# Input projections of a hybrid attention/state-space layer: loads on SyncE's queue, stores on ScalarE's, a third sum tile, and v's second columns after two products

## The chip, the cores and the metric

The kernel runs on one core of one Trainium2 chip. The metric is the time on the device in microseconds (us); a time is the median of several runs. Five engines work side by side, each through its own instructions in order: TensorE (PE, matrix products, with a weight load ahead of each), VectorE (DVE), ScalarE (ACT), GpSimd (POOL) and SyncE (SP), which here only starts transfers (DMAs). ScalarE can start transfers too; such a start stands in its queue among its other instructions, and waits there for what it needs, as they do.

## The reference

One layer on 2048 tokens of 1024 features, all in float32:

```python
h = rms_norm(x, norm_gain)
z = h @ w_in                       # 1024 x 5120
q, k, v, gate_a, u_s, gate_s, merge_logits = split(z)
q, k = rms_norm(q per sub-head), rms_norm(k per sub-head)
o_a = diff_attention(q, k, v, ...) * silu(gate_a)
o_s = s5_branch(u_s, ...) * silu(gate_s)
g_a, g_s = split(sigmoid(merge_logits + merge_gate_b))
x + (g_a * (o_a @ proj_attn) + g_s * (o_s @ proj_ssm)) @ w_out
```

q, k, v, gate_a, u_s and gate_s have 512 columns each, the merge logits 2048. The attention has four heads with two sub-heads of 64 features.

## The kernel before

Each product is made of three, as both factors are split into a coarse part in a short float format (`hh`, `w[0]`) and the rest (`hl`, `w[1]`): high by high, high by low, low by high (`split3`, L38 to L42). A product here is 128 columns of `w_in` by a block of 512 tokens, over 8 slices of the 1024 features: 24 matmuls of 128x512 into one PSUM bank (`proj1`, L206). v is made the other way round, 128 tokens by 256 columns, 24 matmuls of 128x256 (`value`, L250).

The first phase, `phase1`, makes z in this order:

- The input of block t, `load_x` (L167): eight tiles `xs` (tag "x", four buffers) are loaded; ScalarE makes `hh`, VectorE `hl`, ScalarE squares (tag "q", two buffers), GpSimd adds the squares up in `acc` (tag "t", two buffers, L175 and L177). `acc` is split (`sh`, `sl`, tag "s"), summed over the partitions by two matmuls with a matrix of ones (`msx`, L194 and L195), and gives `E` and, for each token, the factor `rc` (L201) that v's evacuation needs (L260).
- Two groups g of q and v columns, four blocks of tokens t in each. In a block, `qk` makes two q products with v's products between them: `n` (L288) says how many of the block's four v's come after the first and after the second. In group 0 the next block's input is made between these products. After the first product the norm of the block before is done (`later`, L229): `ms` (L235, L236), `tt` (tag "t", L238), logarithm and exponential on ScalarE and three operations on VectorE (`newton`, L91), then the two halves of q (L244): the first into a further tile of tag "t", the second into `tt` itself. Each half is split (`hilo`, a cast on ScalarE, a subtraction on VectorE, L864 and L866), and both parts are stored (L247, L248).
- Weights come through raw tiles (`wraw`, three buffers, 256 KB a load): for v by `load_w` (L126; load L135, cast L139, rest L140), for all other columns by `steps_w1` (L150; load L156, cast L160, rest L161). v's weights fill all four buffers of their tag, so the second group's overwrite the first's.
- Two groups of k with the state-space input u (`state`, L303; store L310) in the place of v.
- After `mid()`, which makes the state-space branch, 24 columns of gates (`gate`, L335): product, a factor, Silu or Tanh, store (L352).

All PSUM tiles of these products share six banks (L111); `msx` and `ms` have two of their own. Weight loads, and input loads from block 1 on, are started by ScalarE; all stores, and the input loads of block 0, by SyncE. The order of the instructions on each engine isn't the order of the text: a list scheduler with a model of the times works it out when the program is built, and so mixes v's products into q's, or the state-space branch into the gates. Buffers of a tag are handed out in the order of the text.

Of the kernel before, what the change touches and what calls it, by code (L numbers as in the profile page):

```python
# [17 lines left out]
NTB = 4  # L18
# [26 lines left out]
def block_ones(nc, k, c, bo):  # L45
    nc.gpsimd.memset(bo, 0.0)
    for i in range(0, 128, 32):
        nc.gpsimd.memset(bo[i:i + 32, i:i + 32], 1.0 / 64)
    k.bones = c.tile([128, 128], F32R, name="bones")
    nc.vector.tensor_copy(k.bones, bo)  # L50
    nc.gpsimd.memset(bo, 1.0)
    nc.vector.tensor_copy(k.ones, bo)


def consts(tc, k, I):
    nc = tc.nc
    nc.scalar.preload_act_table_set("natural_log_exp_and_others")
    c = k.cp
    k.ident = c.tile([128, 128], F32, name="ident")
    k.ones = c.tile([128, 128], F32R, name="ones")  # L60
    with tc.tile_pool(name="c0", bufs=1, side="right", reuse_waits="tile") as c0:
        block_ones(nc, k, c, c0.tile([128, 128], F32, name="bo"))
    small = c.tile([128, 8 + 2 + 2 + 16 + 1 + 4], F32, name="small")
    nc.sync.dma_start(small, I["small"])
    k.gain = small[:, 0:8]
    k.qg = c.tile([128, 2], F32, name="qg")
    nc.vector.tensor_scalar(out=k.qg, in0=small[:, 8:10], scalar1=-0.125, scalar2=None, op0=ALU.mult)
    k.kg = small[:, 10:12]
    k.hmb = c.tile([128, 16], F32, name="hmb")
    nc.vector.tensor_scalar(out=k.hmb, in0=small[:, 12:28], scalar1=0.5, scalar2=None, op0=ALU.mult)  # L70
    k.sgain = c.tile([128, 1], F32, name="sgain")
    nc.vector.tensor_scalar(out=k.sgain, in0=small[:, 28:29], scalar1=0.8 * 128 ** 0.5, scalar2=None, op0=ALU.mult)
    k.mhalf = c.tile([128, 2], F32, name="mhalf")
    nc.gpsimd.memset(k.mhalf, -0.5)
    k.hglub = c.tile([128, 4], F32, name="hglub")
    nc.vector.tensor_scalar(out=k.hglub, in0=small[:, 29:33], scalar1=0.5, scalar2=None, op0=ALU.mult)
# [25 lines left out]
def phase1(tc, k, I, mid):  # L102

    nc = tc.nc
    with ExitStack() as es:
# [13 lines left out]

        BUFS = {"x": 4, "s": 2, "q": 2, "t": 2, "n": 2, "o": 2, "v": 2}  # L120
        W = {}
# [4 lines left out]
        def load_w(g, eng=None):  # L126

            W[g] = []
            for i in range(4):
# [4 lines left out]
                o = slice(2 * (i % 2), 2 * (i % 2) + 2)  # L134
                nc.scalar.dma_start(raw, I["win"][g][:, 2 * i:2 * i + 2])  # L135
                if eng:
# [13 lines left out]
        def steps_w1(c, tag, eng=None):  # L150
            w = wh, wl = [k.wp.tile([128, 8, 128], F32R, tag=tag, bufs=4, name="w1") for _ in range(2)]
            yield w
            for i in range(2):
                raw = k.wp.tile([128, 4, 128], F32, tag="wraw", bufs=3, name="wraw")
                o = slice(4 * i, 4 * i + 4)
                nc.scalar.dma_start(raw, I["win"][c // 2][:, o, 128 * (c % 2):128 * (c % 2) + 128])  # L156
                if eng:
# [9 lines left out]
        def load_x(t):  # L167
# [11 lines left out]
            for kk in range(8):  # L179
                xs[kk] = et("x", "xs")  # L180
                (nc.scalar if t else nc.sync).dma_start(xs[kk], I["xT"][kk * 128:(kk + 1) * 128, t * TB:(t + 1) * TB])
                gc = k.gain[:, kk:kk + 1]
# [10 lines left out]
            hilo(nc, sh, acc, sl)  # L193
            nc.tensor.matmul(ms, k.ones, sh, start=True, stop=False)  # L194
            nc.tensor.matmul(ms, k.ones, sl, start=False, stop=True)  # L195
            e, r = E[:, t * TB:(t + 1) * TB], rc[:, 4 * t:4 * t + 4]
# [12 lines left out]

        def qk(w, t, gcol, dst, between):  # L210


            ps, sq = [], []
            for i in range(2):
                ps.append(pm.tile([128, TB], F32, tag="pm", name="ps_qk"))
                proj1(w[i], t, ps[i])
                sq.append(et("q", "sq"))
                nc.scalar.activation(out=sq[i], in_=ps[i], func=AF.Square)
                between(i)
                if i == 0:  # L220
                    later()
            nc.vector.tensor_tensor(out=sq[0], in0=sq[0], in1=sq[1], op=ALU.add)
            sh, sl = et("s", "sh", F32R), et("s", "sl", F32R)
# [5 lines left out]
        def later():  # L229
            if pending:  # L230
                pending.pop()()

        def qk_norm(t, gcol, dst, ps, sh, sl):
# [8 lines left out]
            for i in range(2):  # L242
# [3 lines left out]
                hilo(nc, qh, q, eng=nc.vector)  # L246
                nc.sync.dma_start(f(dst[i, 0, :, :, ts]), f(qh))  # L247
                nc.sync.dma_start(f(dst[i, 1, :, :, ts]), q)  # L248

        def value(g, b):  # L250
# [9 lines left out]
            nc.scalar.activation(out=v, in_=ps.rearrange("p (h d) -> p h d", h=2), func=AF.Copy, scale=rc[:, b:b + 1])  # L260
            nc.sync.dma_start(k.VT[g - 4][:, :, b].rearrange("h p d -> p h d"), v)

# [5 lines left out]
        with ExitStack() as e1:  # L268
# [13 lines left out]
            for g in range(2):  # L282
# [3 lines left out]
                for t in range(NTB):  # L286
                    x = load_x(t + 1) if g == 0 and t + 1 < NTB else iter(())
                    n = (4, 0) if t == NTB - 1 else (2, 2)  # L288
                    b = iter(range(4 * t, 4 * t + 4))
# [6 lines left out]

                    qk(w, t, k.qg, k.QT[g], between)

            for g in range(2, 4):
# [3 lines left out]
                def state(i, t):  # L303
# [5 lines left out]
                    nc.vector.tensor_tensor(out=u[:, ::-1].rearrange("p a c -> p c a"), in0=v(ps), in1=v(R), op=ALU.mult)  # L309
                    nc.sync.dma_start(k.US[2 * (g - 2) + i][:, :, 64 * t:64 * t + 64], u)  # L310

# [23 lines left out]
        def gate(c, ts, w=None, ps=pst):  # L335

            w = w or load_w1(c, "wh" if c == cols[0] else "wl")
            for t in ts:
# [12 lines left out]
                if t == ts[-1] or t % 2:  # L351
                    nc.sync.dma_start(dst[:, t0 * TB:(t + 1) * TB], z[:, 0:t + 1 - t0])  # L352
            return w
# [880 lines left out]
```

## Time and profile before

| | |
|---|---|
| median of 3 runs | 1773.14 us (1772.15 to 1774.92) |
| profiled execution | 1772.99 us, its span 1771.2 us |
| TensorE busy | 1691.9 us, 96% of the span |
| VectorE, ScalarE, GpSimd busy | 1032.2, 699.7, 285.8 us |
| mean granted TensorE clock | 0.986 of full speed |
| moved by DMA | 239.05 MB, 135 GB/s |

The profile is one execution. Stages by what TensorE does: q and v to about 246 us, k and u to about 419 us, the gates to about 990 us (with the state-space branch between them), then the attention and the projections of the result. A wait row reads: the engine and line that waited, the engine and line that ended the wait, total us, number of waits, the longest. A timeline row reads: start and duration in us, engine, line, operation, result and operands; a bracket at its end is idle time of that engine just before.

### The profile page before, as it was taken

To read this page: it belongs to the slowest core of one execution; us is meant where nothing else is said; L and a number is where in the kernel's file an instruction comes from. 1 tells how busy PE (TensorE), PEld (TensorE's weight loads), DVE (VectorE), ACT (ScalarE), POOL (GpSimd) and SP (SyncE) were. 2 spreads that over 40 slices of the span, in tenths; PEclk is the share of its full clock that TensorE was granted. 3 is DMA by queue.
4 is the path that set the end of the run, shared out by engine and by line. 5 is a ranking of instruction groups with operands and counts; after the bars stand their busy time and mean duration, and the time that the engine had idled before them with its cause. 6 is when DMAs were issued, how large, how long until landed. Compare 5 with 4: busy or idle time off the path is not lost.

```text
span 1771.2 us, 24819 instructions
## 1 busy us (share of the span) xinstructions
PE 1691.9 (96%) x8720; PEld 1426.8 (81%) x8720; DVE 1032.2 (58%) x2564; ACT 699.7 (40%) x1426; POOL 285.8 (16%) x428
## 2 busy tenths in 40 slices
PE   7877999999999999999999789999999989999999
PEld 6776988888878788888888668878888879888887
DVE  7533345545734359999644587687677668643331
ACT  4533232324312243331144577675555466511100
POOL 3421000000260000000023335552111032100000
PEclk9888999999999999999999899999999999999999
DMA  5333233424343433323465764753754534654532
GB/s 166 94 92 97 67 107 78 114 76 117 103 127 121 130 119 115 110 95 100 131 203 190 237 202 144 230 169 110 221 173 127 160 103 131 196 162 148 149 101 83
DMA packets 225405, 239.05 MB, mean 135 GB/s; under 512 B 56032, under 2 KB 166016, under 8 KB 224256
## 3 DMA queue, kind: packets, MB, share of 16 engines
q1 hardware_dynamic: 182656, 210.19, 39.1%
q10 hardware_dynamic: 42624, 27.27, 5.4%
q8 instruction: 69, 1.13, 0.3%
q14 instruction: 56, 0.46, 0.1%
HBM read 146.44 MB, written 90.96 MB: 134 GB/s over the span
## 4 chain that ended last, share of the span: by engine, by line
PE 70%; DMA 13%; DVE 7%; ACT 3%; POOL 3%; issue 3%; SPq 1%; ACTq 0%; POOLq 0%; DVEq 0%
PE ps_p L40 9%; PE ps_p L41 9%; PE ps_p L42 9%; PE ps_o L575 5%; PE ps_o L40 3%; PE ps_o L42 3%; PE ps_o L41 3%; PE ps_s L536 2%; PE ps_s L535 2%; PE ps_qk L40 2%; PE ps_qk L41 2%; PE ps_qk L42 2%; PE ps_t L567 2%; DMA xs<-xT 2%; PE ps_u L42 1%
## 5 line engine op out<-in xcount | busy, mean ns | idle before, releaser
L42 PE MATMUL ps_p<-hh,w 128*128 128x512 f32 x768 | 300.3, 391 | 0.0
L40 PE MATMUL ps_p<-hh,w 128*128 128x512 f32 x768 | 300.2, 391 | 0.0
L41 PE MATMUL ps_p<-hl,w 128*128 128x512 f32 x768 | 300.1, 391 | 0.0
L41 PEld LDWEIGHTS ps_p<-hl,w 128*128 128x128 f32 x768 | 144.2, 188 | 30.1 <-issue 0.7
L42 PEld LDWEIGHTS ps_p<-hh,w 128*128 128x128 f32 x768 | 144.3, 188 | 29.5 <-issue 0.4
L40 PEld LDWEIGHTS ps_p<-hh,w 128*128 128x128 f32 x768 | 144.3, 188 | 29.0 <-issue 0.5
L548 ACT ACTIVATE e<-e,mm 128x640 f32<-128x640 f32 (+11 forms) x96 | 136.2, 1419 | 60.5 <-DVE mm L546 59.6
L575 PE MATMUL ps_o<-V,at 128*128 128x128 f32 x1088 | 149.9, 278 | 2.9 <-ACT sq L581 2.2
L575 PEld LDWEIGHTS ps_o<-V,at 128*128 128x128 f32 x1088 | 143.0, 194 | 9.7 <-ACT sq L581 2.8
L535 PE MATMUL ps_s<-K,Q 128*128 128x512 f32 (+3 forms) x320 | 129.5, 408 | 10.4 <-DMA Q<-Q 5.9
L538 DVE TENSOR_SCALAR_CACHE_REDUCE e<-ps_s 128x512 f32<-128x512 f32 (+1 forms) x192 | 120.4, 641 | 27.6 <-PE ps_s L536 26.5
L40 PE MATMUL ps_qk<-hh,w 128*128 128x512 f32 x256 | 102.5, 400 | 15.6 <-ACT hh L183 8.4
L536 PE MATMUL ps_s<-K,Q 128*128 128x512 f32 (+3 forms) x320 | 115.7, 365 | 1.2 <-DMA Q<-Q 1.1
L344 DVE TENSOR_TENSOR z<-ps_p,E 128x512 f32<-128x512 f32 x96 | 66.1, 688 | 75.2 <-PE ps_p L42 74.3
L41 PE MATMUL ps_qk<-hl,w 128*128 128x512 f32 x256 | 102.3, 400 | 4.2 <-DVE hl L184 4.2
L42 PE MATMUL ps_qk<-hh,w 128*128 128x512 f32 x256 | 101.4, 396 | 0.0
L350 ACT ACTIVATE z<-z,hmb 128x512 f32<-128x512 f32 x64 | 46.2, 723 | 124.3 <-DVE z L344 111.8
L567 PE MATMUL ps_t<-ident,e 128*128 128x128 f32 x544 | 84.7, 273 | 9.1 <-DVE e L558 3.8
L558 DVE SCALAR_TENSOR_TENSOR e<-e,cf 128x128 f32<-128x128 f32 (+7 forms) x64 | 90.1, 1407 | 1.2
L256 PE MATMUL ps_v<-w,hh 128*128 128x256 f32 x256 | 75.7, 298 | 10.2 <-ACT w L139 6.8
L569 ACT COPY at<-ps_t 128x512 f32<-128x512 f32 (+3 forms) x160 | 78.8, 520 | 16.7 <-PE ps_t L567 16.5
L567 PEld LDWEIGHTS ps_t<-ident,e 128*128 128x128 f32 x544 | 65.7, 141 | 22.0 <-ACT at L569 6.0
(346 smaller groups left out, 3691.8 us busy)
## 6 DMA issues: line engine op xcount, KB each, us to landing
wraw<-win ACTq DMA_DIRECT2D x80, 256.0 KB
TM<-z SPq DMA_DIRECT2D x32, 512.0 KB
u<-US SPq DMA_DIRECT2D x64, 128.0 KB
K<-K SPq DMA_DIRECT2D x8, 1024.0 KB
Q<-Q SPq DMA_DIRECT2D x32, 256.0 KB
Q<-Q SPq DMA_DIRECT2D x64, 128.0 KB
t<-TM SPq DMA_DIRECT2D x32, 256.0 KB
MS<-t SPq DMA_DIRECT2D x32, 256.0 KB
```

What stands on the lines that cost most here:

```text
L40: nc.tensor.matmul(out, wh, xh, start=start, stop=False)
L41: nc.tensor.matmul(out, wh, xl, start=False, stop=False)
L42: nc.tensor.matmul(out, wl, xh, start=False, stop=stop)
L256: nc.tensor.matmul(ps, xh, wh, start=kk == 0, stop=False)
L535: nc.tensor.matmul(ps, Q[:, 0, s, 128 * b:128 * b + 128], Kt[s][:, ks], start=True, stop=False)
L536: nc.tensor.matmul(ps, Q[:, 1, s, 128 * b:128 * b + 128], Kt[s][:, ks], start=False, stop=True)
L538: nc.vector.tensor_scalar(out=et[:, ks], in0=ps, scalar1=0.0, scalar2=3e38, op0=ALU.add, op1=ALU.min, accum_out=mc[:, i:i + 1])
L548: nc.scalar.activation(out=et, in_=et, func=AF.Exp, bias=mm, scale=-1.0, accum_out=su)
L558: nc.vector.scalar_tensor_tensor(out=e[0], in0=e[1], scalar=cf, in1=e[0], op0=ALU.mult, op1=ALU.add)
L567: nc.tensor.transpose(pt[:, x], e[:, o:o + 128], k.ident)
L569: nc.scalar.copy(AT[g][:, :w], pt[:, :w])
L575: nc.tensor.matmul(po, AT[x // 4][:, x % 4], Vt[x // 8][:, x % 8], start=x == 0, stop=x == n - 1)
```

## The change

- Input and weight loads (L135, L156, L181) are all started by SyncE; the stores of q and k (L247, L248), v (L261), u (L310) and gates (L352) by ScalarE.
- Tag "t" gets a third buffer. The matrix of ones keeps 32 of its 128 columns, and `msx` reads its first column 128 times over.
- In block 0 of the second group, both q products come before all four v's (`n` is (0, 4), not (2, 2)), and the norm of the block before is done after the second product, ahead of the v's.

```diff
--- before.py
+++ after.py
@@ -49,7 +49,7 @@
     k.bones = c.tile([128, 128], F32R, name="bones")
     nc.vector.tensor_copy(k.bones, bo)
     nc.gpsimd.memset(bo, 1.0)
-    nc.vector.tensor_copy(k.ones, bo)
+    nc.vector.tensor_copy(k.ones, bo[:, 0:32])
 
 
 def consts(tc, k, I):
@@ -57,7 +57,7 @@
     nc.scalar.preload_act_table_set("natural_log_exp_and_others")
     c = k.cp
     k.ident = c.tile([128, 128], F32, name="ident")
-    k.ones = c.tile([128, 128], F32R, name="ones")
+    k.ones = c.tile([128, 32], F32R, name="ones")
     with tc.tile_pool(name="c0", bufs=1, side="right", reuse_waits="tile") as c0:
         block_ones(nc, k, c, c0.tile([128, 128], F32, name="bo"))
     small = c.tile([128, 8 + 2 + 2 + 16 + 1 + 4], F32, name="small")
@@ -117,7 +117,7 @@
         E = rp.tile([128, T], F32, name="E")
         rc = k.cp.tile([128, 16], F32, name="rc")
 
-        BUFS = {"x": 4, "s": 2, "q": 2, "t": 2, "n": 2, "o": 2, "v": 2}
+        BUFS = {"x": 4, "s": 2, "q": 2, "t": 3, "n": 2, "o": 2, "v": 2}
         W = {}
 
         def et(tag, name, dtype=F32):
@@ -132,7 +132,7 @@
                     W[g].append((wh, wl))
                 raw = k.wp.tile([128, 2, 256], F32, tag="wraw", bufs=3, name="wraw")
                 o = slice(2 * (i % 2), 2 * (i % 2) + 2)
-                nc.scalar.dma_start(raw, I["win"][g][:, 2 * i:2 * i + 2])
+                nc.sync.dma_start(raw, I["win"][g][:, 2 * i:2 * i + 2])
                 if eng:
                     eng.tensor_copy(wh[:, o], raw)
                 else:
@@ -153,7 +153,7 @@
             for i in range(2):
                 raw = k.wp.tile([128, 4, 128], F32, tag="wraw", bufs=3, name="wraw")
                 o = slice(4 * i, 4 * i + 4)
-                nc.scalar.dma_start(raw, I["win"][c // 2][:, o, 128 * (c % 2):128 * (c % 2) + 128])
+                nc.sync.dma_start(raw, I["win"][c // 2][:, o, 128 * (c % 2):128 * (c % 2) + 128])
                 if eng:
                     eng.tensor_copy(wh[:, o], raw)
                 else:
@@ -178,7 +178,7 @@
 
             for kk in range(8):
                 xs[kk] = et("x", "xs")
-                (nc.scalar if t else nc.sync).dma_start(xs[kk], I["xT"][kk * 128:(kk + 1) * 128, t * TB:(t + 1) * TB])
+                nc.sync.dma_start(xs[kk], I["xT"][kk * 128:(kk + 1) * 128, t * TB:(t + 1) * TB])
                 gc = k.gain[:, kk:kk + 1]
                 nc.scalar.activation(out=hh[t][:, kk], in_=xs[kk], func=AF.Copy, scale=gc)
                 nc.vector.scalar_tensor_tensor(out=hl[t][:, kk], in0=xs[kk], scalar=gc, in1=f(hh[t][:, kk]),
@@ -191,8 +191,8 @@
             ms = k.pF.tile([128, TB], F32, tag="F", bufs=k.NF, name="msx")
             sh, sl = et("s", "sh", F32R), et("s", "sl", F32R)
             hilo(nc, sh, acc, sl)
-            nc.tensor.matmul(ms, k.ones, sh, start=True, stop=False)
-            nc.tensor.matmul(ms, k.ones, sl, start=False, stop=True)
+            nc.tensor.matmul(ms, k.ones[:, 0:1].to_broadcast([128, 128]), sh, start=True, stop=False)
+            nc.tensor.matmul(ms, k.ones[:, 0:1].to_broadcast([128, 128]), sl, start=False, stop=True)
             e, r = E[:, t * TB:(t + 1) * TB], rc[:, 4 * t:4 * t + 4]
             nc.vector.tensor_scalar(out=e, in0=ms, scalar1=EPS / 1024, scalar2=EPS * EPS, op0=ALU.mult, op1=ALU.add)
             sq = et("q", "sq")
@@ -207,7 +207,7 @@
             for kk in range(8):
                 split3(nc, ps, w[0][:, kk], w[1][:, kk], hh[t][:, kk], hl[t][:, kk], kk == 0, kk == 7)
 
-        def qk(w, t, gcol, dst, between):
+        def qk(w, t, gcol, dst, between, last=0):
 
 
             ps, sq = [], []
@@ -216,9 +216,12 @@
                 proj1(w[i], t, ps[i])
                 sq.append(et("q", "sq"))
                 nc.scalar.activation(out=sq[i], in_=ps[i], func=AF.Square)
-                between(i)
                 if i == 0:
+                    between(i)
+                if i == last:
                     later()
+                if i:
+                    between(i)
             nc.vector.tensor_tensor(out=sq[0], in0=sq[0], in1=sq[1], op=ALU.add)
             sh, sl = et("s", "sh", F32R), et("s", "sl", F32R)
             hilo(nc, sh, sq[0], sl, nc.vector)
@@ -244,8 +247,8 @@
                 nc.vector.scalar_tensor_tensor(out=q, in0=ps[i], scalar=gcol[:, i:i + 1], in1=tt, op0=ALU.mult, op1=ALU.mult)
                 qh = et("o", "qh", F32R)
                 hilo(nc, qh, q, eng=nc.vector)
-                nc.sync.dma_start(f(dst[i, 0, :, :, ts]), f(qh))
-                nc.sync.dma_start(f(dst[i, 1, :, :, ts]), q)
+                nc.scalar.dma_start(f(dst[i, 0, :, :, ts]), f(qh))
+                nc.scalar.dma_start(f(dst[i, 1, :, :, ts]), q)
 
         def value(g, b):
             t, o = b // 4, (b % 4) * 128
@@ -258,7 +261,7 @@
                 nc.tensor.matmul(ps, xl, wh, start=False, stop=kk == 7)
             v = k.ep.tile([128, 2, 128], F32, tag="v", bufs=BUFS["v"], name="v")
             nc.scalar.activation(out=v, in_=ps.rearrange("p (h d) -> p h d", h=2), func=AF.Copy, scale=rc[:, b:b + 1])
-            nc.sync.dma_start(k.VT[g - 4][:, :, b].rearrange("h p d -> p h d"), v)
+            nc.scalar.dma_start(k.VT[g - 4][:, :, b].rearrange("h p d -> p h d"), v)
 
         def steps(it, n=1):
             for _ in range(n):
@@ -285,7 +288,7 @@
                     steps(load_w(5), 4)
                 for t in range(NTB):
                     x = load_x(t + 1) if g == 0 and t + 1 < NTB else iter(())
-                    n = (4, 0) if t == NTB - 1 else (2, 2)
+                    n = (4, 0) if t == NTB - 1 else (0, 4) if g and not t else (2, 2)
                     b = iter(range(4 * t, 4 * t + 4))
 
                     def between(i):
@@ -294,7 +297,7 @@
                             value(4 + g, next(b))
                         steps(x, 1 + 8 * i)
 
-                    qk(w, t, k.qg, k.QT[g], between)
+                    qk(w, t, k.qg, k.QT[g], between, int(n[0] == 0))
 
             for g in range(2, 4):
                 w = [load_w1(2 * g + i, "wh") for i in range(2)]
@@ -307,7 +310,7 @@
                     proj1(wu[i], t, ps)
                     v = lambda x: x.rearrange("p (c a) -> p c a", a=8)
                     nc.vector.tensor_tensor(out=u[:, ::-1].rearrange("p a c -> p c a"), in0=v(ps), in1=v(R), op=ALU.mult)
-                    nc.sync.dma_start(k.US[2 * (g - 2) + i][:, :, 64 * t:64 * t + 64], u)
+                    nc.scalar.dma_start(k.US[2 * (g - 2) + i][:, :, 64 * t:64 * t + 64], u)
 
                 for t in range(NTB):
                     R = et("x", "R")
@@ -349,7 +352,7 @@
                     dst = k.TM[c - 24]
                     nc.scalar.activation(out=zi, in_=zi, func=AF.Tanh, scale=0.5, bias=k.hmb[:, c - 24:c - 23])
                 if t == ts[-1] or t % 2:
-                    nc.sync.dma_start(dst[:, t0 * TB:(t + 1) * TB], z[:, 0:t + 1 - t0])
+                    nc.scalar.dma_start(dst[:, t0 * TB:(t + 1) * TB], z[:, 0:t + 1 - t0])
             return w
 
         cols = (12, 13, 14, 15, 20, 21, 22, 23, *range(24, 40))
```

## The prediction

> **What bounds the kernel now.** I read the page first: TensorE (PE) and its granted clock in tenths, each digit a fortieth of the span, some 44 us.
>
> ```profile
> span 1771.2 us, 24819 instructions
> ...
> PE   7877999999999999999999789999999989999999
> ...
> PEclk9888999999999999999999899999999999999999
> ```
>
> PE is at 9 nearly everywhere; the weak places are the first four digits and the two at about 1000 us. The same in numbers, from the busy times by stretches (columns: stretch, its length, then busy us and instruction count of PE, weight loads, VectorE, ScalarE, GpSimd, then clock, DMA share, GB/s), first by stage, then for the weak part of the first:
>
> ```profile
> core 0: us, PE busy (x) PEld busy (x) DVE busy (x) ACT busy (x) POOL busy (x), PEclk, DMA share, GB/s
> 0.00:246.00 246.00, 208.70 (x1196) 182.95 (x1197) 107.82 (x184) 98.70 (x178) 49.93 (x47) 0.94 0.37 104
> 246.00:419.00 173.00, 173.00 (x763) 143.00 (x762) 91.22 (x134) 47.14 (x83) 0.00 (x0) 1.00 0.36 95
> 419.00:990.00 571.00, 568.69 (x2649) 470.28 (x2649) 353.37 (x1021) 187.60 (x350) 73.10 (x100) 1.00 0.43 132
> ```
>
> ```profile
> 20.00:160.00 140.00, 113.77 (x637) 99.37 (x637) 63.03 (x116) 62.06 (x114) 42.16 (x32) 0.89 0.37 107
> ```
>
> All that the diff touches lies in the projections and gates, up to 990 us. From 246 us PE is busy 741.7 of 744 us there: nothing to win, only to lose. The stretch that can give time is 20 to 160 us, the normalised input, q's first columns and v. There PE stands 140 - 113.8 = 26.2 us, and its clock is 0.89, so 0.11 x 113.8 = 12.5 us more go in slow matmuls: 38.7 us in all. The first 20 us I leave out. Who made PE stand (columns: engine and line that waited, releaser, total us, times, longest):
>
> ```profile
> PE ps_qk L40 <- ACT v L260: 7.3, 2, 6.4
> PE ps_v L256 <- ACT w L139: 6.8, 2, 4.9
> PE ps_v L256 <- ACT v L260: 3.4, 1, 3.4
> PE msx L194 <- ACT sh L864: 2.9, 2, 1.8
> PE msx L195 <- POOL sl L866: 1.9, 3, 0.9
> PE ps_qk L40 <- ACT hh L183: 1.5, 1, 1.5
> PE ps_v L257 <- POOL w L140: 1.3, 2, 1.0
> PE ms L236 <- DVE sl L866: 1.0, 1, 1.0
> ```
>
> The rows add up to 26.1, the whole of it. I put them in three causes. **Ring**: the first row, 7.3 us. **Weights of v's second columns**: L139 and L140, 8.1 us. **Input sums**: the other five, 10.7 us. The clock loss follows the gaps: after each, the clock falls for some us.
>
> ```profile
> 64.00:68.00 4.00, 4.00 (x19) 4.00 (x20) 3.76 (x4) 1.97 (x4) 1.72 (x1) 0.50 0.66 133
> 84.00:88.00 4.00, 4.00 (x22) 3.72 (x22) 4.00 (x14) 1.98 (x5) 0.00 (x0) 0.64 0.10 9
> ```
>
> So I charge each us of gap 12.5 / 26.1 = 0.48 us of clock: a factor of 1.48. Ring 10.8, weights 12.0, sums 15.8.
>
> On this clock the Trainium skill speaks ("TensorE: Matmul & The Clock Gate", section "What's actually happening"): the gate closes only after an idle window of about 3.4 us, and stays closed about as long. By that rule only the three longest gaps would pay a half-speed window of about 1.7 us each, 5 us in all, and the two that the forecast below removes would pay 3.4 us, not 7.4, so that it would be 4 us smaller. The row at 84 us, 0.64 after two gaps that were each under 2 us, speaks against so clean a line.
>
> **Third tile for sums and values.** The tag "t" holds the input's sum (acc), the norm's value (tt) and the first half of q. With two tiles they wait for each other and for the stores out of them. VectorE's timeline:
>
> ```profile
> 64.74 0.69 DVE L99 SCALAR_TENSOR_TENSOR tt<-nw_a,nw_y 128x512 f32<-128x512 f32 x1
> ...
> 83.77 0.74 DVE L244 SCALAR_TENSOR_TENSOR q<-ps_qk,qg,tt 128x512 f32<-128x512 f32 x1
> ...
> 86.71 0.68 DVE L866 TENSOR_TENSOR q<-q,qh 128x512 f32<-128x512 f32 x1
> ...
> 87.74 0.68 DVE L866 TENSOR_TENSOR tt<-tt,qh 128x512 f32<-128x512 f32 x1
> ```
>
> The waits of VectorE (20 to 165 us) and of ScalarE (0 to 165 us):
>
> ```profile
> DVE tt L238 <- DMA Q<-tt: 11.3, 1, 11.3
> DVE w L161 <- ACT w L160: 9.1, 2, 5.3
> DVE tt L238 <- DMA Q<-q: 8.6, 1, 8.6
> ```
>
> ```profile
> ACT hh L183 <- DMA xs<-xT: 20.9, 17, 4.1
> ACT nw_y L95 <- DVE tt L238: 10.7, 3, 8.4
> ACT w L139 <- DMA wraw<-win: 9.3, 3, 4.8
> ACT acc L175 <- DMA Q<-q: 7.8, 1, 7.8
> ACT hh L183 <- DVE w L137: 4.9, 3, 3.0
> ```
>
> tt is ready at 65.4, but q is made at 83.8, because its tile is still the next block's sum. Then the stores of both must land before acc (7.8) and tt (11.3) of later blocks can start; ScalarE takes its queue in order, so v's evacuation (L260) comes late and PE, out of PSUM banks, waits. That is the 6.4 us, and the same a block later, tt waiting 8.6 and ScalarE's nw_y behind it 8.4, makes the 0.9 left of the row. With three tiles the order acc, acc, acc, tt, q gives q a tile that the first block's sum left long ago, and the stores have a whole block, over 20 us, to land. I take all of the ring away: -10.8. Bounds: 0 if some other wait stands right behind it, and -10.8 less 2.7 x 1.48 = 4.0 more if the two msx gaps of the last block (1.8 and 0.9 are the longest of their rows) go with it, as that block's sum began 7.8 us late. What is late next: the input's sums, which are costed below.
>
> **v's second columns half a product later.** In the first block of the second group both q products now come before the four v's. The weights of v's second columns reuse the tiles of the first, so their casts can't start before the last v of the first group; the row of L139 shows that ScalarE stood 9.3 us for their loads as well, 4.8 at a time: three raw tiles, two of them held by the q columns' weights. The edit puts one product more in front. A product is 24 matmuls; in the second stretch above, where PE never stands, 763 instructions took 173.0 us, 0.227 each, so 24 x 0.227 = 5.4 us of cover against 8.1 us of waits. The other 2.7 us: these casts stand on ScalarE behind the nw_y that the ring held for 8.4 us, so the ring's end gives back more than that. I take the weights' whole 12.0 away; bounds -8.0 (5.4 x 1.48) and -12.0. The previous block's norm is put off with it (later() after the second product): two PSUM banks stay taken 5.4 us longer, of six, and the four v's that would need them come after it. Nothing.
>
> **Loads to SyncE.** 24 input loads and 80 weight loads leave ScalarE's queue. ScalarE no longer stands where such a load waits for its buffer; it stands where the data is late. In the rows of L183 the 4.9 us, where the load in front waited for VectorE, go. The 20.9 us mostly stay: the input has four tiles before and after, and a load can only start when a square has freed one, on whichever queue it stands. What the gaps of the sums (15.8) lose is therefore between 0 and all; I take -2, the nearest row being the 4.9, of which the part before 20 us gives nothing here. On SyncE the loads now queue behind each other alone: input tile 4 of the first block waits for VectorE, with weight loads behind it; before, the weights were on the other queue. I take 0, bounds -1 and +2. The rule against this edit is in the Trainium skill ("DMA: Bandwidth & Descriptors", section "Issuing engines are not separate DMA queues"): transfers interleave on the same 16 DMA engines whatever queue starts them, and only issue time is saved. By it the -2 would be 0 and the sum 2 us higher. No run shown so far can separate the two.
>
> **Stores to ScalarE.** Per norm four stores, per v, u and gate one. A store of ScalarE's own result waits for its end only. But the second and fourth wait for VectorE's subtraction. ScalarE's casts ahead of them:
>
> ```profile
> 84.55 0.62 ACT L864 CAST qh<-q 128x512 fp32r<-128x512 f32 x1 [0.59 <-DVE q L244]
> ...
> 86.41 0.62 ACT L864 CAST qh<-tt 128x512 fp32r<-128x512 f32 x1
> ```
>
> By these and VectorE's two subtractions above, qh ends at 85.17, the subtraction at 87.39, 2.2 us; then 87.03 to 88.42, 1.4 us. Behind them on ScalarE stand the next casts, input tiles, squares and v. That is 3.6 us a norm, where ScalarE is the link that the sums run through: four norms in the first group, 14.4 us. Most of it falls where ScalarE is idle (62.1 busy of 140): I take +4, bounds 0 and 14.4 x 1.48 = 21.3. From 246 us ScalarE is busy 47.1 of 173 and then 187.6 of 571, PE has six banks of cover: 0. SyncE in turn no longer stands before the state-space loads; PE is full there: 0.
>
> **Shorter ones.** The sums of the input use the shorter tile of ones:
>
> ```profile
> L194 PEld LDWEIGHTS msx<-sh,ones x4: 186/186/188, 27.8 to 118.9; 128*128 128x128 f32 x4
> ```
>
> Four times two such weight loads now read one column broadcast; even at twice the price 8 x 0.19 = 1.5 us, in the gaps. I take 0.
>
> **Sum.** -10.8 - 12.0 - 2 + 4 = -20.8 on the profiled execution's own 1772.99 us (its span 1771.2 and 1.8 around it; the runs' median is 1773.14, the same within 0.2): 1752.2, say **1752 us**. After 160 us everything hangs on PE's order, so it all moves forward together: the state-space work starts when this stage gives its tiles back, and the weak stretch at 1000 us comes as much earlier.
>
> **Rivals.** About 0.2%, 3.5 us, is what a measurement here can tell from no change.
>
> *A, the forecast*: ring and weights go, sums stay. Its own range 1744 to 1761. Chance 0.52.
>
> *B, the sums go too*: q made 18 us earlier frees PSUM, ScalarE freed of loads makes the input tiles in time, and all 38.7 us go but the stores' 4: 1738. For it: 20.9 us of ScalarE waiting for input. Against: the four input tiles and the square's two tiles are as before, and the x sum is emitted in the same place of PE's order. Chance 0.14.
>
> *C, half is given back*: only one of the two is gained, as the other's stall is taken over by the sums (the next block's sum is no earlier than before), or the stores cost half their bound: -20.8 + 10 gives 1762. Chance 0.14.
>
> *D, nothing*: the stores' upper 21.3 eats the 22.8: 1771. This is also the case that the change doesn't do what it says, for instance because the order of each engine's instructions, worked out anew for the changed queues, puts the input loads behind weight loads that wait for a tile. Chance 0.08.
>
> *E, slower*: ScalarE stands before VectorE's subtractions in the second group as well. Of the 16 norms of q and k, each exposed one costs 3.6 x 1.48 = 5.3; the gain of 24.8 without the stores' term is used up from the fifth exposed one on. With eight exposed, 42.6: 1773.0 - 24.8 + 42.6 = 1791. For it: one in-order queue now holds casts, logarithms and waiting stores. Against: PE full for 741.7 of 744 us with ScalarE a third busy. Chance 0.12.
>
> **How the numbers follow.** Faster by over 0.2%: A, B and C, 0.80. Same: D, 0.08. Slower: E, 0.12. The range takes in A, B and C: from B's 1738 to 1768, C with the rest of the stores' bound.
>
> **What would show it.** Right: no wait of tt or acc for a store of q; q within 2 us of tt in the first block; PE's waits for L139 and L140 under 1 us; PE idle in 20 to 140 us down from 26 to about 11 us, at msx, ms and v after an input sum; the first state product at about 225 instead of 246 us; PE full from there to about 970. Wrong: waits of ScalarE, or of the store queue, for the subtraction (L866) over 10 us in the first 140 us with hh or v behind them; PE gaps between 246 and 990 us; or a hand-over at 1000 us with more than the idle time it has now.

## The result and the profile after

The change is faster, by less than forecast: 1760.38 us as the median of 4 runs (1755.97 to 1762.6), beside 1772.89 us for the kernel before on the same chip. The ratio is 0.9925, 95% interval 0.9903 to 0.9946, that is 13.3 us of 1773 (9.6 to 17.2). The profiled execution took 1762.6 us, its span 1760.7. Line numbers from L210 on are 1 to 3 higher than before: `later` calls L238 and L239, q is made at L247, v evacuated at L263, the split stands at L867 and L869.

In the page's rows of TensorE and of its clock, the fourth digit of the first row rose from 7 to 9, the second and fourth of the clock by one each, and the weak place at about 1000 us stayed:

```profile
span 1760.7 us, 24771 instructions
...
PE   7879999999999999999999799999999999999998
...
PEclk9989999999999999999999899999999999999999
```

The stretches of the first stage, with the columns of the prediction:

```profile
0.00:246.00 246.00, 217.04 (x1240) 191.09 (x1241) 116.30 (x193) 100.65 (x182) 50.77 (x47) 0.94 0.38 110
20.00:160.00 140.00, 122.83 (x700) 109.08 (x700) 71.86 (x128) 63.86 (x118) 40.96 (x30) 0.90 0.39 110
```

Between 20 and 160 us PE stands 140 - 122.8 = 17.2 us where it stood 26.2. But the clock is 0.90, where it was 0.89: by the prediction's reckoning 0.10 x 122.8 = 12.3 us go in slow matmuls, about as many as before (12.5). Who makes PE stand there:

```profile
PE ps_v L259 <- ACT v L263: 7.6, 3, 3.4
PE msx L194 <- ACT sh L867: 7.6, 2, 7.4
PE ms L239 <- DVE sl L869: 1.2, 2, 0.7
PE msx L195 <- POOL sl L869: 0.6, 1, 0.6
PE ms L238 <- ACT sh L867: 0.2, 1, 0.2
```

The row of the ring (ps_qk, 7.3) and those of v's weights (L139 and L140, 8.1) are gone; what is left, 17.2 us, are the sums and the v behind them, 10.7 before. VectorE's timeline shows the ring open: tt is ready at 65.5, and q follows at 67.1, not 18 us later.

```profile
64.77 0.69 DVE L99 SCALAR_TENSOR_TENSOR tt<-nw_a,nw_y 128x512 f32<-128x512 f32 x1
...
67.07 0.74 DVE L247 SCALAR_TENSOR_TENSOR q<-ps_qk,qg,tt 128x512 f32<-128x512 f32 x1
```

ScalarE's waits up to 165 us have a new kind, "issue": time in which it waits for nothing that the profile shows, here right behind stores in its own queue.

```profile
ACT hh L183 <- issue: 4.2, 1, 4.2
ACT acc L175 <- DMA Q<-q: 3.4, 1, 3.4
...
ACT v L263 <- issue: 3.1, 1, 3.1
...
ACT sq L175 <- issue: 2.5, 2, 2.1
```

Those are 9.8 us of standing that did not exist before (its waits there had no row of "issue"), on the engine that the sums run through. The obvious reading is that the stores on ScalarE ate the missing 8 us. It was my first theory, and it fell.

### The profile page after: what moved, and what is told of

Read it like the earlier page. It is cut to its first block, busy times and chain, and to the rows that moved or that the text cites. A ratio compares the mean times of both kernels' runs of the same rounds, so it can differ in the third digit from the quotient of the medians.

```text
span 1760.7 us, 24771 instructions
## 1 busy us (share of the span) xinstructions
PE 1693.2 (96%) x8720; PEld 1433.1 (81%) x8720; DVE 1027.7 (58%) x2564; ACT 702.6 (40%) x1426; POOL 284.0 (16%) x428
## 4 chain that ended last, share of the span: by engine, by line
PE 68%; DMA 13%; DVE 6%; ACT 4%; POOL 4%; issue 3%; SPq 1%; ACTq 0%; POOLq 0%; DVEq 0%
PE ps_p L40 9%; PE ps_p L42 9%; PE ps_p L41 9%; PE ps_o L578 3%; PE ps_o L42 3%; PE ps_o L40 3%; PE ps_o L41 3%; PE ps_qk L41 3%; PE ps_qk L42 3%; PE ps_qk L40 3%; PE ps_a L40 2%; PE ps_a L41 2%; PE ps_a L42 2%; PE ps_u L40 2%; PE ps_u L41 2%
## 5 line engine op out<-in xcount | busy, mean ns | idle before, releaser
L544 DVE CUSTOM_DVE_ANT_0 e<-ps_s,nb 128x384 f32<-128x384 f32 (+3 forms) x128 | 70.0, 553 | 19.5 <-PE ps_s L539 15.7
```

## The experiments

All ratios are to runs of the kernel before on the same chip. The groups ran on different chips, so ratios are to be compared across them, not medians. "us" is (ratio - 1) x 1773; "u" is the start of the first state product in the profiled execution.

| kernel | ring | v's columns | loads | stores | median us | ratio, 95% interval | us | u |
|---|---|---|---|---|---|---|---|---|
| the change | new | new | SP | ACT | 1760.38 | 0.9925 (0.9903 to 0.9946) | -13.3 | 236.5 |
| e1 | new | | ACT | SP | 1752.02 | 0.9877 (0.9857 to 0.9896) | -21.8 | 233.7 |
| e2 | | new | ACT | SP | 1767.30 | 0.9970 (0.9956 to 0.9983) | -5.3 | 244.3 |
| e3 | new | new | ACT | SP | 1752.13 | 0.9879 (0.9862 to 0.9896) | -21.5 | 232.2 |
| e4 | | | SP | ACT | 1771.02 | 0.9987 (0.9973 to 1.0001) | -2.3 | 242.7 |
| e5 | new | new | SP | SP | 1757.35 | 0.9906 (0.9889 to 0.9924) | -16.7 | 238.7 |
| e6 | new | new | ACT | ACT | 1769.81 | 0.9978 (0.9963 to 0.9992) | -3.9 | 241.1 |
| e8 | new | new | SP | q, k: SP; rest ACT | 1765.51 | 0.9953 (0.9938 to 0.9969) | -8.3 | 238.1 |
| e9 | own sum tile | | ACT | SP | 1766.64 | 0.9963 (0.9949 to 0.9976) | -6.6 | 240.3 |
| e10 | new | new | ACT | q, k, v: ACT; rest SP | 1770.49 | 0.9976 (0.9963 to 0.9988) | -4.3 | 243.4 |
| e11 | new | new | ACT | u, gates: ACT; rest SP | 1766.53 | 0.9953 (0.9935 to 0.9970) | -8.3 | 230.6 |
| e12 | new | new | SP | ACT, order of e3 | 1754.94 | 0.9885 (0.9864 to 0.9906) | -20.4 | 233.1 |
| e13 | new | new | ACT | SP, order of the change | 1759.29 | 0.9913 (0.9897 to 0.9929) | -15.4 | 237.7 |

### The parts one by one (e1 to e4)

e1 is the kernel before with the third tile (and the short tile of ones that makes room for it); e2 only has v's columns half a product later; e3 has both, on the old queues; e4 has only the loads and stores moved.

```diff
-        BUFS = {"x": 4, "s": 2, "q": 2, "t": 2, "n": 2, "o": 2, "v": 2}
+        BUFS = {"x": 4, "s": 2, "q": 2, "t": 3, "n": 2, "o": 2, "v": 2}
```

> The third tile of tag t alone (with the shorter tile of ones that goes with it), all queues and v's order as before. Theory T, that the ring and the weights' wait bring the gain and the stores on ScalarE take part of it back: the wait of 11.3 us of tt for a store is gone, PE's longest gap of 6.4 us with it, the weights' gaps near 145 us stay: 7 to 11 us faster, about 1764. Rival R, that the gain is the work of the queues: within 3 us of before, 1770 to 1773.

```diff
-                    n = (4, 0) if t == NTB - 1 else (2, 2)
+                    n = (4, 0) if t == NTB - 1 else (0, 4) if g and not t else (2, 2)
-                    qk(w, t, k.qg, k.QT[g], between)
+                    qk(w, t, k.qg, k.QT[g], between, int(n[0] == 0))
```

> v's second columns after both products alone, queues and two tiles as before. Theory T: PE's gaps at L139 and L140 (8.1 us and their clock) shrink, the ring's 6.4 us stay: 5 to 12 us faster, about 1764. Rival R: within 3 us of before.

> Third tile and v's later columns together, loads on ScalarE and stores on SyncE as before. Theory T: ring and weights are gone and nothing stands before the stores on ScalarE: 18 to 24 us faster than before, about 1752, so 6 to 10 us faster than the whole change. Rival R: 3 to 6 us faster than before at most, about 1768, slower than the whole change's 1760.

```diff
-                nc.scalar.dma_start(raw, I["win"][g][:, 2 * i:2 * i + 2])
+                nc.sync.dma_start(raw, I["win"][g][:, 2 * i:2 * i + 2])
...
-            nc.sync.dma_start(k.VT[g - 4][:, :, b].rearrange("h p d -> p h d"), v)
+            nc.scalar.dma_start(k.VT[g - 4][:, :, b].rearrange("h p d -> p h d"), v)
```

> Loads to SyncE and stores to ScalarE alone, two tiles and v's order as before. Theory T: the ring's waits for the stores stay, and ScalarE stands behind stores that wait: 0 to 10 us slower than before, 1773 to 1783. Rival R: 8 to 13 us faster, about 1762.

The third tile alone brings 21.8 us, more than the whole change and twice what was expected of it; v's columns alone bring 5.3, and on top of the third tile nothing (e3 beside e1). The queues alone bring nothing that can be told from no change, which neither theory had. Each of these kernels has its own order of instructions, which is counted in here (e9, and the last section of experiments). PE's waits of e1 between 20 and 165 us say why the second edit is idle:

```profile
PE msx L194 <- ACT sh L864: 6.4, 1, 6.4
PE ps_v L256 <- ACT v L260: 6.1, 3, 3.4
PE ms L236 <- DVE sl L866: 1.9, 2, 1.2
PE ps_qk L40 <- ACT hh L183: 1.1, 2, 0.8
PE ps_v L257 <- POOL w L140: 0.7, 2, 0.5
```

No row of L139, and 0.7 us of L140, although v's columns stand where they stood before. In the kernel before, ScalarE waits 8.4 us for tt ahead of these casts; in e1 it waits 0.7. So the casts were late, in the main, because they stood on ScalarE behind the norm that the ring held up, and in e1 nothing is left for the cover of half a product to hide. In e4, where the ring is closed, the row is there:

```profile
PE ps_v L256 <- ACT v L260: 8.4, 2, 5.0
PE ps_v L256 <- ACT w L139: 6.3, 2, 5.8
```

So of the change's three parts one, with the order that comes with it, does the work, and the question is why ring and columns with the new queues (the change, -13.3) bring 8 us less than with the old ones (e3, -21.5).

### Which of the moved transfers (e5, e6, e8)

e5 is e3 with the loads on SyncE, e6 is e3 with the stores on ScalarE, e8 is the change with the four stores of q and k back on SyncE:

```diff
-                nc.scalar.dma_start(f(dst[i, 0, :, :, ts]), f(qh))
-                nc.scalar.dma_start(f(dst[i, 1, :, :, ts]), q)
+                nc.sync.dma_start(f(dst[i, 0, :, :, ts]), f(qh))
+                nc.sync.dma_start(f(dst[i, 1, :, :, ts]), q)
```

> The whole change but for the stores, which stay on SyncE: third tile, v's later columns, loads on SyncE. Loads and stores now share SyncE's queue. Theory T2, that the 8 us which the whole change loses against third tile plus later columns (1752) are ScalarE standing at the stores it starts: 1750 to 1754. Rival R2, that the loads lose them, standing in SyncE's one queue behind weight loads that wait for a tile: 1758 to 1764, or worse, as stores stand there too.

> The whole change but for the loads, which stay on ScalarE: ScalarE starts loads and stores. Theory T2: 1758 to 1764, ScalarE standing some 10 us at stores (issue, and casts behind a store) in the first 160 us. Rival R2: 1750 to 1754.

> The whole change, but q's and k's four stores a norm start on SyncE again; v's, u's and the gates' stay on ScalarE. Theory T2 with its cause at the stores that wait for VectorE's subtraction: most of the 8 us come back, 1751 to 1755. If it is ScalarE's time at any store: 1756 to 1759. Rival R2: no better than 1760, since these stores join the loads' queue.

The loads alone cost 4.8 us beside e3, the stores alone 17.6, both together 8.2; and with the stores of q and k, at which ScalarE mostly stood, taken away again (e8) the kernel is 5 us slower than the change, not faster. No price for each transfer makes these four numbers, and e5 and e6 fit neither theory. The standing of ScalarE can't be the whole of it.

### A tile of its own for the sums (e9)

With three tiles the last block's sum still waits for a store. e9 has the same memory split otherwise: the sums have one tile of their own, tt and q share the other two.

```diff
-                    acc = et("t", "acc")
+                    acc = et("a", "acc")
-        BUFS = {"x": 4, "s": 2, "q": 2, "t": 2, "n": 2, "o": 2, "v": 2}
+        BUFS = {"x": 4, "s": 2, "q": 2, "t": 2, "a": 1, "n": 2, "o": 2, "v": 2}
```

> Queues and v's order as before; the same three tiles as the third-tile run, but one is the input sums' own (tag a, one buffer), two are tt's and q's. In the third-tile run the last input sum still waits 4.2 us for q's store, ScalarE in front of the rest of block 2's sum, and PE then stands 6.4 us at msx. If that wait is what is left of the ring: it goes, and 3 to 9 us with it, 1743 to 1749. If one buffer makes the next sum wait for the one before instead: 1752 or slower.

A miss: it is 15 us slower than the shared three. The second branch covers that time, but the wait that it names is 0.7 us in the trace (acc behind the subtraction of L866). The wait for v's weights is back:

```profile
PE msx L194 <- ACT sh L864: 6.0, 1, 6.0
PE ps_v L256 <- ACT v L260: 4.9, 2, 3.0
PE ps_v L256 <- ACT w L139: 3.8, 1, 3.8
```

Here the norm isn't held up: the last of these casts waits 4.5 us for its load, which ScalarE starts at 140.6 us, in e1 at 136.9. So the place of the load in the order counts as well as the ring.

No sum waits for a store in e9, and the msx gap is as long as with that wait (6.0 beside 6.4 in e1). So the store that the last sum waits for does not by itself make this gap; what does is open. Nor is the tile all that differs between e9 and e1. Compared instruction by instruction in the traces, PE's order in e9 is that of the kernel before but for some 30 of 8720, all in the first 200 us. In e1 some 570 stand elsewhere, nearly all of them between 1000 and 1300 us, in the attention, where neither edit touches a line. How much of the 15 us is the tile's and how much the order's is open.

### Early stores or late ones (e10, e11)

e10 is e3 with the stores of q, k and v alone on ScalarE, e11 with those of u and the gates alone:

```diff
-                    nc.sync.dma_start(k.US[2 * (g - 2) + i][:, :, 64 * t:64 * t + 64], u)
+                    nc.scalar.dma_start(k.US[2 * (g - 2) + i][:, :, 64 * t:64 * t + 64], u)
-                nc.sync.dma_start(dst[:, t0 * TB:(t + 1) * TB], z[:, 0:t + 1 - t0])
+                nc.scalar.dma_start(dst[:, t0 * TB:(t + 1) * TB], z[:, 0:t + 1 - t0])
```

> Third tile and v's columns as in the change, loads on the old queues, and only the stores of q, k and v (L250, L251, L264) on ScalarE; u's and the gates' stay on SyncE. With all stores on ScalarE the time was 1769.8, with none 1752.1. Theory T3: the loss of a store on ScalarE is made in the projections, where ScalarE stands before a store with casts, squares and input tiles behind it: here 1762 to 1770 us, the first state product at about 241 us rather than 232. Rival R3: it is made by the gates' stores, which stand in front of the next factor's or tile's work on ScalarE: here 1751 to 1756 us, the first state product at about 232.

> The other half: only the stores of u and of the gates (L313, L355) on ScalarE, those of q, k and v on SyncE. T3: 1752 to 1757 us, as without any store on ScalarE; at most the 4 us by which the gates' stage was longer with all of them there. R3: 1762 to 1770. If both halves come out near 1752, or both near 1765, the loss is no sum over stores, and the order that is worked out anew for each set of queues is what differs.

Each half costs about as much as all of them: 17.2 and 13.2 us beside e3, all together 17.6 (e6). Each run by itself fits one theory, e10 T3 and e11 R3; together they fit neither, but the third case that e11's expectation names. e11 is even the earliest of all at its first state product (230.6) and loses it all later. What the five kernels e5, e6, e8, e10 and e11 have in common is that the list scheduler works out a new order of the engines' instructions for each set of queues: in their traces 11 to 25% of PE's instructions stand elsewhere than in e3, in the change 27%.

### The same queues in the other order (e12, e13)

So the last two hold the order. After the text is traced, each instruction of TensorE, VectorE, ScalarE and GpSimd is chained, as an order of issue without a wait, to the one ahead of it in another kernel's order; transfers stay free. The traces bear it out: all 8720 of PE's instructions and all 1426 of ScalarE's stand in e12 in the order of e3, and in e13 in that of the change; of VectorE's and GpSimd's a handful stand elsewhere. e12 has the change's queues in e3's order, e13 e3's queues in the change's order.

```diff
+            i = tc.nc.get_inst_by_name(f"I-{at}")
+            if last is not None:
+                tc.add_manual_dep(i, last.name, why, reason="order")
+            last = i
```

> The whole change, with the order of instructions pinned: TensorE, VectorE, ScalarE's computations and GpSimd take the order that was worked out for the third tile and v's columns with the old queues (that kernel ran 1752.1 us; with its own order the change ran 1760.4). Only the transfers stand on other queues. Theory O: what the queues cost is the other order that is worked out for them, so here 1750 to 1754 us, first state product at about 232 us. Theory Q: it is ScalarE standing at stores, whatever the order: 1758 to 1763, the first state product at 236 or later, and waits of ScalarE for nothing that the profile shows (issue) of some 10 us before 165 us. In between: both.

> The reverse: third tile and v's columns on the old queues, loads on ScalarE and stores on SyncE, with the four engines pinned to the order that was worked out for the whole change. Theory O: 1758 to 1764 us. Theory Q: 1750 to 1754 us.

| ratio (span of the profiled execution) | order of e3 | order of the change | what the order costs |
|---|---|---|---|
| old queues | 0.9879 (1750.0) | 0.9913 (1756.8) | 0.0034, 6.0 us |
| the change's queues | 0.9885 (1753.1) | 0.9925 (1760.7) | 0.0040, 7.1 us |
| what the queues cost | 0.0006, 1.1 us | 0.0012, 2.1 us | |

Of the 8.2 us, 6 to 7 go with the order and 1 to 2 with the queues. That is theory O, though e12's median lies 0.9 us above its range. By the intervals of the ratios each of these differences is uncertain by 4 to 5 us: the order's part is clear of zero with either set of queues, the queues' part isn't in either order. The single spans put the queues at 3 to 4, and the order at 7 to 8. The starts of the state products (first time of each row) show the same grouping by order: e3 and e12 together, e13 and the change together.

```profile
L40 PE MATMUL ps_u<-hh,w x48: 389/389/389, 232.2 to 292.9; 128*128 128x512 f32 x48
```

```profile
L40 PE MATMUL ps_u<-hh,w x48: 389/389/389, 233.1 to 293.8; 128*128 128x512 f32 x48
```

```profile
L40 PE MATMUL ps_u<-hh,w x48: 389/389/389, 237.7 to 298.4; 128*128 128x512 f32 x48
```

```profile
L40 PE MATMUL ps_u<-hh,w x48: 389/389/389, 236.5 to 297.2; 128*128 128x512 f32 x48
```

These are e3, e12, e13 and the change. And ScalarE stands behind its stores in e12 for even longer than in the change, 4.3 + 3.1 + 2.9 + 2.5 = 12.8 us up to 165 us, while the kernel is 7 us faster:

```profile
ACT sq L175 <- issue: 4.3, 2, 2.5
...
ACT v L263 <- issue: 3.1, 1, 3.1
ACT w L139 <- issue: 2.9, 1, 2.9
...
ACT hh L183 <- issue: 2.5, 1, 2.5
```

With 12.8 us of standing e12 is 1.1 us slower than e3, within the noise. My first theory, that the standing is the missing 8 us, is refuted by it.

Where the order makes PE stand can be read too. All of PE's gaps of over 1 us between 85 and 110 us, of the change, of e13 and of e12:

```profile
91.25 0.80 PE L194 MATMUL msx<-sh,ones 128*128 128x512 f32 x1 [7.35 <-ACT sh L867]
...
102.08 0.39 PE L259 MATMUL ps_v<-w,hh 128*128 128x256 f32 x1 [2.26 <-ACT v L263]
```

```profile
92.68 0.80 PE L194 MATMUL msx<-sh,ones 128*128 128x512 f32 x1 [6.96 <-ACT sh L867]
...
103.69 0.39 PE L259 MATMUL ps_v<-w,hh 128*128 128x256 f32 x1 [2.24 <-ACT v L263]
```

```profile
90.54 0.80 PE L194 MATMUL msx<-sh,ones 128*128 128x512 f32 x1 [6.01 <-ACT sh L867]
```

In the change's order, on either queues, v's first matmul behind the input sum waits 2.2 to 2.3 us for a PSUM bank; in e12 that wait is 0.4. An older v can leave its bank only once `rc` of its block is known, which comes out of `msx`:

```profile
101.36 0.16 DVE L99 SCALAR_TENSOR_TENSOR rc<-nw_a,nw_y 128x4 f32<-128x4 f32 x1
```

The change's order puts the last of v's matmuls and two of the q product ahead of msx. In e3's order four of v's matmuls and the whole of the next q product stand behind msx and help to cover the 10 us from msx (91.25 in the change) to rc. It is a matter of a handful of matmuls, and this gap is open in both kernels that have the order. The clock pays for it as well, in the change and then in e12:

```profile
100.00:104.00 4.00, 1.92 (x13) 1.92 (x14) 2.47 (x6) 3.08 (x6) 1.60 (x2) 0.89 0.47 131
104.00:108.00 4.00, 4.00 (x26) 4.00 (x26) 3.99 (x6) 1.89 (x5) 0.79 (x1) 0.68 0.25 66
```

```profile
100.00:104.00 4.00, 3.58 (x28) 3.15 (x28) 1.91 (x5) 3.57 (x7) 1.29 (x1) 1.00 0.64 169
104.00:108.00 4.00, 4.00 (x31) 3.78 (x30) 3.98 (x5) 2.39 (x6) 1.28 (x1) 1.00 0.32 85
```

In these 8 us e12 makes 59 matmuls, the change 39. Of the 7 us, 3.4 (e12) to 5.5 (e13) are there by the first state product. Where the rest is not, PE's idle time by stretches shows (length less busy time, in the profiled executions):

| stretch, us | before | e9 | e1 | e3 | e12 | the change | e13 |
|---|---|---|---|---|---|---|---|
| 0 to 160 | 37.3 | 32.2 | 29.5 | 26.3 | 28.0 | 29.0 | 30.2 |
| 160 to 960 | 1.5 | 1.1 | 0.5 | 1.1 | 1.7 | 1.7 | 0.9 |
| 960 to 1180 | 24.3 | 24.6 | 21.7 | 24.4 | 24.0 | 21.1 | 22.1 |
| 1180 to the end | 16.3 | 15.9 | 12.2 | 12.0 | 12.4 | 15.7 | 14.0 |

From 160 to 960 us, k, u and nearly all of the gates, the order costs nothing. From 1180 us on, in the attention and the projections of the result, the change's order stands 2 to 3 us longer than e3's, and before that, around the hand-over at 1000 us, as much less. In sum idle time is the smaller part. The same 8720 instructions keep PE busy 1693.2 us in the change and 1687.0 in e12, at a mean clock of 0.982 and 0.988; 1689.6 in e13 and 1686.1 in e3, at 0.986 and 0.990. So of the 7.6 and 6.8 us between the spans, 6.2 and 3.5 are slower work, and 1.4 and 3.3 more idle time. Over all runs of these kernels the mean clock is 0.984 beside 0.987, and 0.987 beside 0.989. Why it is lower in the change's order is shown for the one place above and was not followed further.

e1 (-21.8), e3 (-21.5) and e12 (-20.4) are the fastest kernels here, and can't be told from each other: the third tile in the order worked out for the old queues.

## Why the prediction came out as it did

The sign and the range held; the forecast of 1752 was 8 us too low. By the steps of the sum:

- **Ring and weights, -22.8**: together -21.5 (e3, with the order worked out for it). The mechanism of the ring was right, as q 2 us behind tt, and no wait of tt for a store, show. The split was wrong: I put 12.0 on the edit that moves v's columns, and in e1, without that edit, their waits are down to 0.7 us: the ring held those casts as well, though not alone (in e9, with no wait for a store left, 4.6 of the 8.1 us remain). The prediction had half of this ("these casts stand on ScalarE behind the nw_y that the ring held"), but used it for 2.7 us only.
- **Where that gain lies** was not as I thought. By the first state product (in the kernel before: the row below) e3 has won 246.5 - 232.2 = 14.3 us, not 22.8. The other 7 come after 960 us, in a part of the kernel that the edits don't touch: up to there PE stands 1.5 us before and 1.1 in e3, and from 1180 us on 16.3 and 12.0. PE's order in e1 and e3 differs from that of before mostly there, and e9, which keeps the order of before, stands 15.9 us there as the kernel before does. So these 7 are likely the order's and not the ring's. No run has the third tile in the order of before, so it isn't shown, and that -21.5 meets -22.8 is partly luck. The change itself has its first state product at 236.5 (forecast 225) and its last gate product at 981.0 (forecast 970).

```profile
L40 PE MATMUL ps_u<-hh,w x40: 389/389/389, 246.5 to 295.7; 128*128 128x512 f32 x40
```

- **The sums, "stays"**: they grew from 10.7 to 15.0 us of idle in e3 and 17.2 in the change. I had said that with three tiles the stores have a whole block to land. For the last block's sum that is false: in the change it takes q's tile, whose store was issued at 71.9, and ScalarE waits for that store until 83.4.

```profile
71.90 0.83 ACTq L251 DMA_DIRECT2D Q<-q  x1
...
83.40 0.63 ACT L175 ACTIVATE acc<-xs 128x512 f32<-128x512 f32 x1 [3.38 <-DMA Q<-q]
```

- **The factor 1.48 for the clock** supposes that slow time goes with idle time. In the change 9.0 us of idle went and next to no slow time (12.5 before, 12.3 after); in e3, with 15.0 of idle, it is 0.06 x 125.0 = 7.5. So the slow time doesn't follow the sum of the gaps.

```profile
20.00:160.00 140.00, 125.03 (x729) 110.41 (x728) 73.72 (x128) 66.20 (x123) 43.51 (x32) 0.94 0.38 110
```

- **The queues, -2 and +4**, together +2: with the order held, loads and stores together cost 1.1 us (order of e3) or 2.1 us (order of the change). That is right in size, within an uncertainty of some 5 us; the two terms were not parted in one order. The upper bound of 21.3 for the stores, and rival E built on the same wait, are borne out by no run. The Trainium skill's rule ("DMA: Bandwidth & Descriptors", section "Issuing engines are not separate DMA queues") is that starting transfers from several engines saves the time of starting them alone; the 1.1 to 2.1 us for the whole exchange agree with it.
- **The step that failed** is the one without a number: I summed the edits in the order that the trace of before shows, and ended with "it all moves forward together". That the order is worked out anew for the changed queues I mentioned once, in rival D, as an accident. It is what cost 6.0 to 7.1 us, the largest error that is left in the sum; those of the ring's term (-21.8 in e1, not -10.8) and of the weights' (nothing on top of it, not -12.0) cancel. With it: -21.5 + 1.1 + 7.1 = -13.3.
- **Case C** gave the number, 1762, for another cause (stores at half their bound, or one gain taken over by the sums). Of the signs that I named as wrong, ScalarE's standing at stores did appear, 9.8 us, though while stores were started and not for the subtraction, and it meant little. A PE gap of 5.3 us between 246 and 990 us appeared too, at 986.7: the hand-over behind the gates, which had moved ahead.
- **The clock gate.** The Trainium skill ("TensorE: Matmul & The Clock Gate", section "What's actually happening") has the gate close only after some 3.4 us of idle. In the change the clock was back at 0.96 from 96 to 100 us, PE then stood for 2.26 us, and from 104 to 108 us the clock was 0.68. That speaks against that line once more, and here it is part of what was lost.

## What to carry to other kernels

Where a scheduler orders the instructions, an edit's effect is the edit plus a new order, and the order can be worth more than the edit: take the order of one variant for the other, both ways round, before a time is put down to a queue or a store. Idle time that appears on another engine is no explanation until a kernel with the same idle time is slow for it. And where two waits stand behind each other on one engine, count them once: open the first, and look whether the second is still there.

## What the runs showed that I had not expected

- Starting a transfer can hold ScalarE for long: 1.7 and 2.0 us for two of the three stores below (ScalarE's queue in the change, around 113 us; start and duration), 0.5 for the one between them, and the next operation stands until they are through. What makes some of them long is not shown. Even so the whole exchange of queues costs 1 to 2 us.

```profile
111.20 1.99 ACTq L251 DMA_DIRECT2D Q<-q  x1
113.23 0.53 ACTq L250 DMA_DIRECT2D Q<-qh  x1
113.80 1.71 ACTq L251 DMA_DIRECT2D Q<-tt  x1
115.56 0.73 ACT L183 ACTIVATE hh<-xs,small 128x512 fp32r<-128x512 f32 x1 [4.20 <-issue]
```

- Five kernels that differ from e3 in their queues alone spread over -16.7 to -3.9 us. For the change, e12 and e13 show that most of such a difference is the order; for the five it is the likeliest reading, and no run tested it.
